# Norm sums made on all partitions, and four sums moved behind a mask, in a two-layer hybrid trunk

## The chip, the cores and the metric

The kernel runs on one core of a Trainium2 chip. The metric is the device time of one execution in microseconds (us). A core has a matrix engine (TensorE, in the profile PE, with its weight loads as PEld), a vector engine (VectorE, DVE), a scalar engine (ScalarE, ACT) that evaluates functions such as Exp or Sqrt from tables it has to load, GpSimd (POOL), and SyncE (SP), which here only issues DMA transfers. Data lie in SBUF with 128 partitions; TensorE writes its products to PSUM banks of 128 x 512 fp32, and a bank can take a new product only when the old one has been read. Every engine works through its own instructions in a fixed order, so an instruction that waits holds up all behind it on that engine.

## The reference

The input is x with 1024 tokens of 1024 channels, fp32. Cut to what matters here:

```python
def rmsnorm(x, g):
    return x * rsqrt(mean(x * x, axis=-1) + EPS) * g

# layer 0: S5 state-space branch with GLU, and retention, each times its gate
u, g_s5, q, k, v, g_ret = split(rmsnorm(x, norm_g[0]) @ w_in_ab)
y_s5 = glu(gelu(s5(u))) * silu(g_s5)
y_ret = retention(q, k, v) * silu(g_ret)      # 8 heads, chunks of 64 tokens
x = x + concat([y_s5, y_ret]) @ w_out_ab

# layer 1: convolution module
a, b, g = split(rmsnorm(x, norm_g[1]) @ w_in_c)
u = depthwise_causal_conv(a * sigmoid(b), width=31) + conv_b
u = (u - mean(u)) * rsqrt(var(u) + EPS) * ln_g + ln_b
x = x + (silu(u) * silu(g)) @ w_out_c

out = rmsnorm(x, final_g)
```

All means run over the 1024 channels of a token. There are three RMS norms and one layer norm over channels (the "conv norm").

## The kernel before

Everything is held with channels on the partitions and tokens along the free dimension: 8 blocks of 128 channels, and two halves of 512 tokens (`HALF`). Each weight product is done as three fp32r products, high x high, high x low and low x high (`mm3`, lines L181 to L183), so one 128 x 512 output block over 1024 channels is 24 matrix products. Norm factors are one number per token. Because the tokens lie along the free dimension, a factor must stand on all 128 partitions, as a 128 x 512 tile, before a block can be multiplied by it.

The order of instructions on each engine is chosen by a scheduler from the program's order, from priorities (`self.at(...)`) and from explicit orderings (`issue_after`). Two names of such orderings are used to hold back weight products until a norm's matrix products have been placed: `self.last_stat` (the last sum) and `self.last_spread` (the last spread).

How a norm's factor is made. ScalarE squares the blocks, GpSimd or VectorE adds the squares of the 8 blocks, which leaves one 128 x 512 tile that must still be summed over the partitions.

- `token_sums` (L444): each 128 x 128 part of that tile is the stationary operand and 64 columns of ones move, in plain fp32. One instruction is two MATMULs in the profile. The sum of token t comes out on partition t, so 512 tokens become a 128 x 4 tile.
- `rsqrt` (L453, L454): Sqrt on ScalarE with its own table, reciprocal on VectorE, on that small tile.
- `spread_split` (L461 to L473) puts the 4 columns on all partitions: they are split into a high and a low part, VectorE multiplies the identity by each (two diagonal 128 x 512 tiles, `dg`), and two fp32r products with ones add them up. `spread` (L480, L483) does it with one plain fp32 diagonal.

Where it happens:

- Layer 0's front (`layer0_front`): the sums of all 1024 tokens (tile `ss`) after the first step of the second half of the u2 product; the factors R (L335) for both halves after two spreads; `Rtok`, the same factors with tokens on partitions, is a by-product that the values of retention use. Then `u_block(nb)` multiplies finished products by R (`ut`, L356, "eviction"), and SP stores each `ut` to `u_d` (L364). `ut` has 2 buffers, so block 2 must wait until block 0's store has read its buffer. The products themselves have three rotating banks beside those of u0 and u1; the second half of u3 takes the bank of u2's first half, and so waits for its eviction. The S5 parameter steps (`s5t`, 128 x 32 and 128 x 64) are VectorE work between them, and the low part of u5's weights (`wl_u`, L172) too.
- Layer 1's norm, for each half (`h1`, names r_ps, r_R), the conv norm for each half (`conv_norm`, cst for its sums of values and of squares, cR for the factor and cD for mean times factor), and the final norm (`final_norm`, rf_ps, rf_R): the first half whole, the second half in two quarters of 256 tokens. For the last quarter `IDLE` products keep TensorE going and the factor is spread twice (rf_R and rf_C).

Retention runs in four pairs of heads (`ret_heads`). For each pair: keys are transposed, kv products per chunk (L1116), the state S chained over the chunks on VectorE (L1124, L1126), scores sp (L1133), masked by VectorE into sc (L1139) in two halves `hf`, then the output ro from S (L1160) and from the masked scores (L1165), statistics (L1174), and transposes back (rt). Beside each pair, `y_pass(rq, pair)` carries a part of the S5 output y through DMA, Gelu, a store to `yn_d`, four in-place sums on VectorE (L917 to L920), and after a `yield` a split into high and low parts with stores to `t_d`. The sums are written in place, so they must wait until the `yn_d` store has read the tiles. For the pairs 1 and 2 the split comes behind the second masked scores.

## Time and profile before

| what | value |
| --- | --- |
| median of 3 runs | 1183.63 us (1182.59 to 1185.37) |
| the profiled execution | 1188.26 us, of which its span is 1186.5 us |
| mean granted TensorE clock | 0.995 of full speed |
| TensorE busy | 1173.5 us (99%), 6326 instructions |
| VectorE busy | 851.1 us (72%), 1479 instructions |
| GpSimd busy | 657.4 us (55%), 448 instructions |
| ScalarE busy | 483.6 us (41%), 712 instructions |
| ScalarE's table loads | 12.8 us in 10 |

A profile page counts in us from the start of the span. In a timeline a row is: start, duration, engine, line, operation, output<-inputs, shapes, and in brackets the idle time before it with what ended it; "x4" says that four equal instructions are drawn together, and their duration is that of the whole group. In the chain of waits a row is start, duration, and what the time went to. Matrix products overlap: one starts before the modelled end of the one before, so costs are taken from starts. The granted clock is the share of TensorE's full speed that its throttle allowed.

### The profile page before, as it was taken

The numbers are of one execution on the slowest core, as the hardware profiler recorded it, in microseconds if no ns is written. First come the engines' busy times: TensorE is split into PE (matmuls) and PEld (weight loads), VectorE is DVE, ScalarE is ACT, GpSimd is POOL, SyncE is SP. The second block draws the span as 40 slices with busy tenths as digits, with TensorE's granted clock in tenths as the row PEclk, the third lists the DMA queues.
The fourth block names the chain that finished last, engine by engine and source line by source line (L and its number), as shares of the span: only waits on it lengthen the run. The fifth ranks groups of instructions, "written<-read, shape, count | busy, mean of one in ns | idle before, by whom it ended". The sixth has DMA issues, their size and how long they took to land.

```text
span 1186.5 us, 17318 instructions
## 1 busy us (share of the span) xinstructions
PE 1173.5 (99%) x6326; PEld 985.8 (83%) x6326; DVE 851.1 (72%) x1479; ACT 483.6 (41%) x712; POOL 657.4 (55%) x448
## 2 busy tenths in 40 slices
PE   9999999999999999899999999999999999999997
PEld 7888888888888889889888888888888888888886
DVE  7975698777427458476679422699999999989743
ACT  6322232222222231333546322545435676434662
POOL 2059999888145354232574110678444567767753
PEclk9999999999999999999999999999999999999999
DMA  9344355565387676759998987655668754357874
GB/s 355 107 129 136 131 156 167 182 186 170 109 280 280 233 231 181 259 177 343 371 344 290 336 266 254 213 198 196 227 243 280 231 180 166 107 189 253 268 246 145
DMA packets 117637, 261.46 MB, mean 220 GB/s; under 512 B 10672, under 2 KB 42288, under 8 KB 116912
## 3 DMA queue, kind: packets, MB, share of 16 engines
q1 hardware_dynamic: 117552, 260.36, 65.4%
q8 instruction: 49, 0.80, 0.3%
q14 instruction: 36, 0.29, 0.1%
HBM read 181.48 MB, written 74.65 MB: 216 GB/s over the span
## 4 chain that ended last, share of the span: by engine, by line
PE 93%; DMA 3%; DVE 2%; issue 1%; SPq 0%; POOL 0%; ACT 0%; POOLq 0%; DVEq 0%; ACTq 0%
PE mm_g L181 8%; PE mm_g L183 7%; PE mm_g L182 7%; PE mm_wo L182 5%; PE mm_wo L181 5%; PE mm_wo L183 5%; PE mm_b L182 2%; PE mm_b L183 2%; PE mm_a L183 2%; PE mm_a L182 2%; PE mm_b L181 2%; PE mm_a L181 2%; PE mm_oc L181 2%; PE mm_oc L183 2%; PE mm_oc L182 2%; PE mm_u L183 2%
## 5 line engine op out<-in xcount | busy, mean ns | idle before, releaser
L1467 DVE SCALAR_TENSOR_TENSOR cv<-u,convw,cv 128x512 f32<-128x512 f32 x398 | 273.7, 751 | 9.0 <-ACT cv L1450 6.9
L1444 POOL TENSOR_TENSOR tp<-tp,tp 128x512 f32<-128x512 f32 x64 | 83.7, 1307 | 35.2 <-ACT tp L1443 34.0
L181 PE MATMUL mm_g<-xh,wh_g 128*128 128x512 f32 x256 | 101.8, 398 | 0.0
L183 PE MATMUL mm_g<-xh,wl_g 128*128 128x512 f32 x256 | 100.1, 391 | 0.0
L182 PE MATMUL mm_g<-xl,wh_g 128*128 128x512 f32 x256 | 100.0, 391 | 0.0
L415 POOL TENSOR_TENSOR s1q<-s1q,s1q 128x512 f32<-128x512 f32 x12 | 17.7, 1478 | 85.2 <-ACT s1q L410 85.2
L1443 ACT ACTIVATE tp<-u,convw 128x512 f32<-128x512 f32 x64 | 45.6, 719 | 37.3 <-POOL tp L1444 35.8
L181 PEld LDWEIGHTS mm_g<-xh,wh_g 128*128 128x128 f32 x256 | 48.0, 188 | 11.7 <-issue 1.2
L183 PEld LDWEIGHTS mm_g<-xh,wl_g 128*128 128x128 f32 x256 | 48.1, 188 | 10.4
L182 PEld LDWEIGHTS mm_g<-xl,wh_g 128*128 128x128 f32 x256 | 48.1, 188 | 9.9 <-issue 0.4
L371 DVE TENSOR_TENSOR gt<-mm_g,R 128x512 f32<-128x512 f32 x32 | 21.9, 684 | 46.5 <-PE mm_g L183 46.4
L172 POOL TENSOR_TENSOR wl_glu<-wf_glu,wh_glu 128x1024 fp32r<-128x1024 f32 x14 | 34.0, 2428 | 33.8 <-ACT wh_glu L171 33.2
L183 PE MATMUL mm_oc<-zh,wl_woc 128*128 128x512 f32 (+1 forms) x144 | 52.5, 366 | 0.0
L172 POOL TENSOR_TENSOR wl_v<-wf_v,wh_v 128x1024 fp32r<-128x1024 f32 x12 | 31.1, 2601 | 38.5 <-ACT wh_v L171 38.5
L182 PE MATMUL mm_oc<-zl,wh_woc 128*128 128x512 f32 (+1 forms) x144 | 52.5, 366 | 0.0
L181 PE MATMUL mm_oc<-zh,wh_woc 128*128 128x512 f32 (+1 forms) x144 | 52.3, 369 | 0.0
L181 PE MATMUL mm_g<-h1h,wh_cg 128*128 128x512 f32 x128 | 49.9, 390 | 0.0
L181 PE MATMUL mm_wo<-ysh,wh_wos 128*128 128x512 f32 x128 | 49.9, 390 | 0.0
L182 PE MATMUL mm_b<-h1l,wh_cb 128*128 128x512 f32 x128 | 49.9, 390 | 0.0
L183 PE MATMUL mm_g<-h1h,wl_cg 128*128 128x512 f32 x128 | 49.8, 389 | 0.0
L181 PE MATMUL mm_b<-h1h,wh_cb 128*128 128x512 f32 x128 | 49.8, 389 | 0.0
L182 PE MATMUL mm_a<-h1l,wh_ca 128*128 128x512 f32 x128 | 49.8, 389 | 0.0
(506 smaller groups left out, 3663.6 us busy)
## 6 DMA issues: line engine op xcount, KB each, us to landing
wf_g<-w_ab SPq DMA_DIRECT2D x16, 512.0 KB
wf_wos<-w_out SPq DMA_DIRECT2D x16, 512.0 KB
wf_wor<-w_out SPq DMA_DIRECT2D x16, 512.0 KB
wf_cb<-w_c SPq DMA_DIRECT2D x16, 512.0 KB
wf_ca<-w_c SPq DMA_DIRECT2D x16, 512.0 KB
wf_woc<-w_out_c SPq DMA_DIRECT2D x16, 512.0 KB
wf_v<-w_v SPq DMA_DIRECT2D x12, 512.0 KB
wf_cg<-w_c SPq DMA_DIRECT2D x11, 512.0 KB
```

Of the source, the lines that this page charges most:

```text
L172: self.low_made = lo[i].tensor_tensor(wl[:].rearrange(fl)[:, c], wf[:, c], h.bitcast(F32), op=ALU.subtract)
L181: nc.tensor.matmul(ps, wh[:, kb, :], xh, start=start, stop=False, **more)
L182: nc.tensor.matmul(ps, wh[:, kb, :], xl, start=False, stop=False, **more)
L183: self.last_mm = nc.tensor.matmul(ps, wl[:, kb, :], xh, start=False, stop=stop, **more)
L371: nc.vector.tensor_tensor(gt[:, c], ps[:], self.R[:, c], op=ALU.mult)
L415: nc.gpsimd.tensor_tensor(a, a, sq[:], op=ALU.add)
L1443: nc.scalar.mul(sk[:], u[:, k:k + HALF], cw[:, nb, k:k + 1])
L1444: gp.tensor_tensor(s0[:], s0[:], sk[:], op=ALU.add)
L1467: v.scalar_tensor_tensor(dst[:], *tap, accs_[i][:], op0=ALU.mult, op1=ALU.add)
```

## The change

All norms but the last quarter of the final one get their sums on all partitions at once: `wide_sums` has a 128 x 128 tile of ones as the stationary operand and moves the 128 x 512 tile of added squares in plain fp32, so each of the 128 output partitions has the sum of every token. `wide_rsqrt` then works on whole tiles: ScalarE does Ln, Exp with scale -0.5, and Square; VectorE does one Newton step in two `scalar_tensor_tensor` passes. It loads the table for Ln and Exp ahead (not for the first half of the conv norm, `table=bool(h)`). The diagonal tiles, the spreads, the tiny `rsqrt` tiles of these norms, and the orderings that held products back for a spread are removed. The conv norm has one bank each for the two sums, and mean times factor is made by one VectorE pass. In the front, the two halves are summed and made into R one after the other, behind the first and the second step of the second half of u2; `Rtok` now comes by DMA: R's first row is written to a new DRAM tile `r_d` and read back as 128 x 8. Both stand on SP's queue ahead of the stores of `ut`. The last quarter keeps the old way (`rstd_last`), with its Sqrt table loaded after the third quarter's Square.

In `y_pass` a second `yield` stands ahead of the four sums. For all pairs but the third (`pair == 2`) the caller goes on at once, as before; for the third, `ret_heads` calls `scored()` after the first half's masks, and there the four sums are issued, behind the first mask.

```diff
@@ -28,11 +28,10 @@
-RMM = 5
-NORM_TAPS = (23, 24), (11, 12)
+NORM_TAP = 23, 11
@@ -214,14 +213,13 @@
-        self.mhalf = self.cp.tile([P, KB], F32, name="mhalf")
-        nc.vector.memset(self.mhalf[:], -0.5)
+        self.r_d = dt("r_d", [1, T])
@@ -262,7 +260,7 @@
-            nc.scalar.activation(sq[:], xt[kb][:], AF.Square)
+            self.squared = nc.scalar.activation(sq[:], xt[kb][:], AF.Square)
@@ -319,26 +317,21 @@
         self.R = self.mid.tile([P, T], F32, name="R0")
         self.Rtok = self.mid.tile([P, 8], F32, name="Rtok")
-        rps = acc[1]
         w_u2 = self.wnext("u2")
         u2 = [self.bank(f"mm_u2_{h}", aux=False) for h in range(2)]
         self.gemm(u2[0][:], w_u2, xs[0])
-        u2_step = lambda kb: self.mm3(u2[1][:], w_u2, kb, (xs[1][kb][0][:], xs[1][kb][1][:]), kb == 0, kb == KB - 1)
-        u2_step(0)
-        with self.tc.issue_after(self.last_mm.ins):
-            self.token_sums([(rps, ssum[:])])
-        self.rsqrt(self.Rtok[:], rps[:].rearrange("p (b x) -> p b x", x=64)[:, :, 0], 1.0 / D)
-        for h in range(2):
-            rp = acc[h]
-            self.spread_split(rp[:], self.Rtok[:, 4 * h:4 * h + 4], ev, f"r0_{h}", (("dg", 2), ("sq", 2)), True)
-            nc.scalar.copy(self.R[:, h * HALF:(h + 1) * HALF], rp[:])
-        r_diag = self.last_diag
-        for kb in range(1, KB):
-            with self.tc.issue_after(self.last_spread.ins) if kb >= RMM else nullcontext():
-                u2_step(kb)
+        for kb in range(KB):
+            self.mm3(u2[1][:], w_u2, kb, (xs[1][kb][0][:], xs[1][kb][1][:]), kb == 0, kb == KB - 1)
+            if kb < 2:
+                c = slice(kb * HALF, (kb + 1) * HALF)
+                with self.tc.issue_after(self.last_mm.ins):
+                    self.wide_sums(acc[kb][:], [ssum[:, c]])
+                self.wide_rsqrt(acc[kb][:], ev, f"r0_{kb}", 1.0 / D, self.R[:, c], bufs=2)
+        r_ready = self.last_newton
+        nc.sync.dma_start(self.r_d[:], self.R[0:1, :])
+        nc.sync.dma_start(self.Rtok[:], self.r_d[0].rearrange("(b p) -> p b", p=P))
         def scaled(nb, w, name, cb):
             for h in range(2):
@@ -376,7 +369,7 @@
-        with self.tc.issue_after(xdma.ins), self.tc.issue_after(r_diag.ins):
+        with self.tc.issue_after(xdma.ins), self.tc.issue_after(r_ready.ins):
@@ -436,78 +429,72 @@
-    def token_sums(self, terms):
...
-    def rsqrt(self, dst, src, scale=1.0, pool=False):
...
+    def wide_sums(self, ps, parts):
+        for i, a in enumerate(parts):
+            self.last_stat = self.nc.tensor.matmul(ps, self.ones[:], a, start=i == 0, stop=i == len(parts) - 1)
+    def wide_rsqrt(self, src, pool, name, scale=1.0, dst=None, copy=None, bufs=1, table=True):
+        nc, v, n = self.nc, self.nc.vector, src.shape[1]
+        half = pool.tile([P, HALF], F32, name=f"{name}_ha", tag="sq", bufs=bufs)[:, :n]
+        y = copy
+        if y is None:
+            y = pool.tile([P, HALF], F32, name=f"{name}_y", tag="dg", bufs=bufs)[:, :n]
+        dst = src if dst is None else dst
+        after = self.squared
+        if table:
+            with self.tc.issue_after(after.ins):
+                after = nc.scalar.preload_act_table_set("natural_log_exp_and_others")
+        with self.tc.issue_after(after.ins):
+            nc.scalar.activation(y, src, AF.Ln, scale=scale, bias=self.epst[:])
+        nc.scalar.activation(y, y, AF.Exp, scale=-0.5)
+        self.halved = nc.scalar.activation(half, y, AF.Square, scale=(0.5 * scale) ** 0.5)
+        v.scalar_tensor_tensor(src, src, EPS / scale, half, op0=ALU.add, op1=ALU.mult)
+        self.last_newton = v.scalar_tensor_tensor(dst, src, 1.5, y, op0=ALU.subtract, op1=ALU.mult, reverse0=True)
+        if copy is not None:
+            nc.scalar.copy(copy, dst)
+    def rsqrt(self, dst, src, scale=1.0):
-    def spread_split(self, ps, r4, pool, name, slots=(("dg", 1), ("sq", 1)), low_scalar=False):
...
-    def spread(self, ps, r4, pool, name, tag="dg", bufs=1, more=()):
...
-    def rstd(self, parts, pool, name, idle=0):
...
+        root = nc.scalar.activation(dst, src, AF.Sqrt, scale=scale, bias=self.epst[:])
+        nc.vector.reciprocal(dst, dst)
+        return root
+    def rstd(self, parts, pool, name, copy=None, table=True):
+        n = parts[0].shape[1]
+        ps = self.bank(f"{name}_R")
+        self.wide_sums(ps[:, :n], parts)
+        self.wide_rsqrt(ps[:, :n], pool, name, 1.0 / D, copy=copy, table=table)
+        return ps
+    def rstd_last(self, parts, pool, name):
+        with self.tc.issue_after(self.halved.ins):
+            nc.scalar.preload_act_table_set("sqrt_and_others")
+        ps, wait, *rp = (self.bank(f"{name}_{k}", aux=False) for k in ("ps", "wait", "R", "C"))
+        terms = [(b, a[:, b * P:(b + 1) * P]) for a in parts for b in range(nb)]
+        for i, (b, a) in enumerate(terms):
+            last = nc.tensor.matmul(ps[:, b * 64:(b + 1) * 64], a, self.ones[:, :64], start=i == 0, stop=i == len(terms) - 1)
+        with self.tc.issue_after(last.ins):
+            for _ in range(IDLE):
+                last = nc.tensor.matmul(wait[:, :P], self.ones[:], self.ones[:], start=True, stop=True)
+        dg = pool.tile([P, 4, P], F32, name=f"{name}_dg", tag="sq", bufs=1)[:, :nb, :]
+        nc.vector.tensor_tensor(dg, self.ident[:].unsqueeze(1).broadcast_to([P, nb, P]),
+                                r4.unsqueeze(2).broadcast_to([P, nb, P]), op=ALU.mult)
+        with self.tc.issue_after(last.ins):
+            for o in rp:
+                nc.tensor.matmul(o[:, :n], self.ones[:], dg.rearrange("p b t -> p (b t)"), start=True, stop=True)
@@ -913,6 +900,7 @@
+        yield
@@ -972,14 +960,22 @@
                     held.enter_context(self.tc.issue_after(self.last_rs.ins))
                 parts = self.y_pass(rq, pair)
                 next(parts)
+                if pair != 2:
+                    next(parts)
                 if pair in (0, 3):
                     next(parts, None)
+            def scored():
+                if pair == 2:
+                    with self.tc.issue_after(self.masked[0].ins):
+                        next(parts)
             def turned():
                 if pair == 3:
                     early.close()
                     self.lp = self.pool("l1", side="right")
-            self.ret_heads(pair, *cur, V, turned)
+            self.ret_heads(pair, *cur, V, turned, scored)
             if pair < 3:
                 with self.tc.issue_after(self.masked[1].ins):
@@ -1139,6 +1135,8 @@
                 self.masked[hf] = v.tensor_tensor(
                     sc[hh][:, 4 * hf:4 * hf + 4, :], sps[hh][:].rearrange("p (b i) -> p b i", b=4),
                     mask[:, hh, :].unsqueeze(1).broadcast_to([P, 4, P]), op=ALU.mult)
+            if hf == 0:
+                scored()
         gts = []
@@ -1459,11 +1457,11 @@
-                    ahead = [x for x, k0 in zip(self.norm_first, NORM_TAPS[i]) if (h, n2) == (0, 6) and k >= k0]
+                    ahead = (h, n2) == (0, 6) and k >= NORM_TAP[i]
-                    with self.tc.issue_after(ahead[-1].ins) if ahead else nullcontext():
+                    with self.tc.issue_after(self.norm_first.ins) if ahead else nullcontext():
@@ -1511,30 +1509,23 @@
         def conv_norm(h):
             sm, acc = accs[("cv", h)]
-            st = ps_cv.tile([P, HALF], F32, name=f"cst_{h}", tag="cn")
+            s1, s2 = (ps_cv.tile([P, HALF], F32, name=f"cst{i}_{h}", tag="cn") for i in range(2))
             q7 = csquare(h, 7)
-            s1, s2 = st[:, 0:256], st[:, 256:512]
             e = v if h else gp
             e.tensor_tensor(sm[:], sm[:], cv[h][7][:], op=ALU.add)
             e.tensor_tensor(acc[:], acc[:], q7[:], op=ALU.add)
-            self.token_sums([(s1, sm[:]), (s2, acc[:])])
-            st4 = st[:].rearrange("p (k b x) -> p k b x", k=2, x=64)
-            t4 = [lp.tile([P, 4], F32, name=f"cn4_{i}_{h}", tag=f"cn4_{i}", bufs=1) for i in range(4)]
-            d4, q4, v4, r4 = (t[:] for t in t4)
-            nc.scalar.activation(q4, st4[:, 0, :, 0], AF.Square, scale=1.0 / D)
-            nc.scalar.mul(d4, st4[:, 0, :, 0], 1.0 / D)
-            v.scalar_tensor_tensor(v4, st4[:, 1, :, 0], 1.0 / D, q4, op0=ALU.mult, op1=ALU.subtract)
-            self.rsqrt(r4, v4)
-            v.tensor_tensor(d4, d4, r4, op=ALU.mult)
-            Rp = ps_cv.tile([P, HALF], F32, name=f"cR_{h}", tag="cn")
-            self.spread_split(Rp[:], r4, lp, f"cR_{h}")
-            Dp = ps_cv.tile([P, HALF], F32, name=f"cD_{h}", tag="cn")
-            with self.tc.issue_after(self.last_diag.ins):
-                self.spread_split(Dp[:], d4, lp, f"cD_{h}", (("tp", 3),) * 2 if h else (("dg", 1), ("sq", 1)))
-            self.norm_mm[h] = self.last_stat, self.last_spread
+            self.wide_sums(s1[:], [sm[:]])
+            first = self.last_stat
+            self.wide_sums(s2[:], [acc[:]])
+            self.norm_mm[h] = first, self.last_stat
+            m2 = lp.tile([P, HALF], F32, name=f"cm2_{h}", tag="dg", bufs=1)
+            self.squared = nc.scalar.activation(m2[:], s1[:], AF.Square, scale=1.0 / D)
+            v.scalar_tensor_tensor(s2[:], s2[:], 1.0 / D, m2[:], op0=ALU.mult, op1=ALU.subtract)
             R = lp.tile([P, HALF], F32, name=f"RL_{h}", tag="cq", bufs=1)
+            self.wide_rsqrt(s2[:], lp, f"cn_{h}", copy=R[:], table=bool(h))
+            Rp = s2
             dl = lp.tile([P, HALF], F32, name=f"dl_{h}", tag="cs", bufs=1)
             for nb in range(8):
                 c = cv[h][nb]
@@ -1543,8 +1534,7 @@
-                    nc.scalar.copy(R[:], Rp[:])
-                    nc.scalar.copy(dl[:], Dp[:])
+                    v.scalar_tensor_tensor(dl[:], s1[:], 1.0 / D, R[:], op0=ALU.mult, op1=ALU.mult)
@@ -1591,13 +1581,15 @@
-            rp = self.rstd([final[h][nb][1][:, c] for nb in ((0, KB - 1) if end else (0,))], lp, f"rf_{h}_{c.start}",
-                           IDLE if end else 0)
+            if end:
+                rp, copied = self.rstd_last([final[h][nb][1][:, c] for nb in (0, KB - 1)], lp, f"rf_{h}_{c.start}")
+            else:
+                rp = self.rstd([final[h][0][1][:, c]], lp, f"rf_{h}_{c.start}", R[:, :n], h == 0)
-                if nb == (4 if end else 1):
-                    nc.scalar.copy(R[:, :n], (self.copied if end else rp)[:, :n])
+                if end and nb == 4:
+                    nc.scalar.copy(R[:, :n], copied[:, :n])
@@ -1615,17 +1607,16 @@
-        self.hold = {4: self.last_stat, 8: self.last_spread}
+        self.hold = {4: self.last_stat}
-        self.norm_first = self.last_sum, self.last_diag
+        self.norm_first = self.last_sum
-            gates((0,), range(G0), {0: {4: self.last_stat, 7: self.last_spread}, 1: {0: self.last_spread},
-                                  2: {0: self.last_spread}})
+            gates((0,), range(G0), {0: {4: self.last_stat}, 1: {0: self.last_stat}, 2: {0: self.last_stat}})
@@ -1655,8 +1646,8 @@
-                stat, spread = self.norm_mm[1]
-                blocks(0, range(N0, 8), {N0: {HOLD: stat}, N0 + 1: {0: spread}})
+                first, stat = self.norm_mm[1]
+                blocks(0, range(N0, 8), {N0: {HOLD: stat}, N0 + 1: {0: stat}})
@@ -1671,10 +1662,9 @@
-                sums, spread = self.last_stat, self.last_spread
+                sums = self.last_stat
-                among.update({0: sums, 3: spread})
+                among.update({0: sums})
```

More of the change, by code (lines that the diff above doesn't have):

```diff
@@ L437, in at @@
         return cm()
-    def token_sums(self, terms):
-        terms = [(ps[:, b * 64:(b + 1) * 64], a[:, b * P:(b + 1) * P]) for ps, a in terms
-                 for b in range(a.shape[1] // P)]
-        for i, (o, a) in enumerate(terms):
-            self.last_stat = self.nc.tensor.matmul(o, a, self.ones[:, :64], start=i == 0, stop=i == len(terms) - 1)
-    def rsqrt(self, dst, src, scale=1.0, pool=False):
-        nc = self.nc
-        if pool:
-            nc.vector.tensor_scalar(dst, src, scale, EPS, op0=ALU.mult, op1=ALU.add)
-            nc.gpsimd.tensor_tensor(dst, dst, self.mhalf[:, :dst.shape[1]], op=ALU.pow)
-        else:
-            root = nc.scalar.activation(dst, src, AF.Sqrt, scale=scale, bias=self.epst[:])
-            nc.vector.reciprocal(dst, dst)
-            return root
@@ L1086, in ret_values_wide, with ret_heads @@
         return lambda p, b, hh: res[b // 4][:, b % 4, (2 * p + hh) * P:(2 * p + hh + 1) * P]
[L1088 removed]
+    def ret_heads(self, pair, K, Q, qadds, mask, kdec, V, turned, scored):
         nc, rp = self.nc, self.rp
```

43 lines of the change are left out of this document (2 added, 41 removed).

## The prediction

> **What bounds the kernel now.** I read the page first: busy time, the chain that ended last, the costliest groups.
>
> ```profile
> PE 1173.5 (99%) x6326; PEld 985.8 (83%) x6326; DVE 851.1 (72%) x1479; ACT 483.6 (41%) x712; POOL 657.4 (55%) x448
> ...
> PE 93%; DMA 3%; DVE 2%; issue 1%; SPq 0%; POOL 0%; ACT 0%; POOLq 0%; DVEq 0%; ACTq 0%
> ...
> L1467 DVE SCALAR_TENSOR_TENSOR cv<-u,convw,cv 128x512 f32<-128x512 f32 x398 | 273.7, 751 | 9.0 <-ACT cv L1450 6.9
> ```
>
> TensorE sets the time: it is busy for 99% and the chain runs on it for 93%. So what counts is TensorE work added or removed, and TensorE's waits. VectorE, at 72%, is nearest to it where the taps of the depthwise convolution run (the last row: 398 of them, with 9.0 us of idle time before them). The view of PE's waits has few (total, times, longest), the largest and the smallest of them:
>
> ```profile
> PE sp L1133 <- DVE S L1126: 3.5, 1, 3.5
> ...
> PE mm_u L181 <- DVE ut L356: 0.3, 1, 0.3
> ```
>
> The first is in the third pair's retention pass, the other in the front, where layer 0's first factors are made. The change touches both. Two views of the first, the chain from 490 us and the granted clock in half microseconds (last three numbers of a row: clock, DMA share, GB/s):
>
> ```profile
> 492.74 6.02 DMA yn_d<-yn
> ...
> 498.88 0.70 DVE yn L917
> ...
> 503.25 1.83 PE sp L1133 x13
> ...
> 505.29 1.42 PE ro L1160 x11
> 506.71 3.29 PE ro L1165 x16
> ```
> ```profile
> 499.50:500.00 0.50, 0.26 (x2) 0.00 (x0) 0.47 (x2) 0.00 (x0) 0.00 (x0) 1.00 0.67 270
> ...
> 502.50:503.00 0.50, 0.00 (x0) 0.00 (x0) 0.46 (x2) 0.00 (x0) 0.00 (x0) 0.57 0.00 0
> ...
> 509.00:509.50 0.50, 0.50 (x5) 0.50 (x5) 0.50 (x4) 0.00 (x0) 0.00 (x0) 0.60 1.06 426
> ```
>
> The four sums of y wait for a DMA until 498.88 and take 0.70 each. The S chain stands behind them on VectorE, and TensorE stands still for 3.5 us before 503.25. Its clock halves at about 502.7, 3.0 us into the stop, and is back at about 509.1, 5.9 us after work resumed. So this wait costs twice. The same work of an earlier pair, at full clock, and, from TensorE's timeline, the start of the weight products ahead of the third pair's sp:
>
> ```profile
> 406.47 0.97 PE sp L1133 x13
> ...
> 407.56 0.67 PE ro L1160 x11
> 408.23 1.98 PE ro L1165 x16
> ```
> ```profile
> 496.48 0.50 PE L181 MATMUL mm_k<-xh,wh_k 128*128 128x512 f32 x1
> ```
>
> The slow clock cost (1.83 - 0.97) + (1.42 - 0.67) + (3.29 - 1.98) = 2.92 us on top of the 3.5.
>
> **Third pass: the four sums behind the first masked scores.** S then needs only kv, which TensorE has behind it before 496.48, so S is ready near 498. In the changed order nine mm_k products (0.23 each) stand ahead of the rest of sp, which starts near 498.6. Both losses go: -3.5 - 2.9 = -6.4. What is late next is the second half's masked scores: on VectorE they queue behind three of the sums, which still start at 498.88, and kraw between them. Three sums, kraw and two masks at 0.65 to 0.70 end at 502.3 (first mask) and 503.0 (second). TensorE has sp and the first half's ro to do, 0.97 + 0.67 + 1.98 = 3.6 us, so to 502.2, and then needs the two banks that the masks free. I price that new wait at 0.6 (0.1 to 0.9: one bank or both). ScalarE has nothing in this; the fourth sum feeds only transposes some 12 us later. Term: **-5.8** (-6.3 to -5.0).
>
> **The norms' sums.** Chain rows of the old way, sums (L444) and spreads (L473), and one row of a plain fp32 product, 256 wide, which is two MATMULs:
>
> ```profile
> 906.46 0.84 PE r_ps L444 x8
> 909.43 0.53 PE r_R L473 x2
> ...
> 1110.36 1.73 PE cst L444 x16
> 1116.96 0.47 PE cR L473 x2
> ...
> 1178.87 0.70 PE L483 MATMUL rf_R<-rf_dg,ones 128*128 128x256 f32 x2
> 1179.40 0.59 PE L483 MATMUL rf_C<-rf_dg,ones 128*128 128x256 f32 x2
> ```
>
> No row shows a plain fp32 product 512 wide. The nearest is the last pair: MATMULs that last 0.379 start 0.21 apart (0.59 - 0.38), so 256 wide costs 0.42 and 512 wide twice that, 0.85. From below: two MATMULs at the spacing of an fp32r one of the same width (0.23: two in 0.47, the cR row) cost 0.45. From above: the rf_R row is followed 0.53 later, which doubled is 1.06. I take 0.85, the same number format. Then each layer-1 norm half and the last norm's first half saves 0.84 + 0.49 - 0.85 = about 0.48 (three: -1.4); each conv norm half has two sums and two spreads, 1.73 + 2 x 0.47 - 1.70 = 0.97 (two: -1.9); the third quarter of the last norm about 0.4. Together **-3.7**; 7.5 wide products outside the front make the ends -6.7 and -2.1.
>
> Cover: the new factor is three ScalarE passes and two VectorE passes over a whole tile, some 0.6 and 0.7 each, about 3.2 us, against tiny passes and diagonal tiles before, a similar length. TensorE covers it with weight products of the other half or the next stage, as it did; without that cover a norm would stop TensorE for those 3.2 us. For the second conv norm the margin is small, by VectorE's timeline:
>
> ```profile
> 1109.35 0.68 DVE L1520 TENSOR_TENSOR cq<-cq,cvq 128x512 f32<-128x512 f32 x1
> ```
>
> The last add ends at 1110.03, the sums run at 1110.36. With the saving of about 2 us ahead of it TensorE would arrive there before VectorE, which has the taps to do. I put 0.5 for these places together (0 to 2).
>
> **The front.** These are VectorE's, TensorE's, ScalarE's and SP's timelines:
>
> ```profile
> 38.99 0.42 DVE L549 TENSOR_SCALAR s_s_ci<-s_s_ci 128x512 f32<-128x512 f32 x1
> ...
> 40.26 0.09 DVE L657 MEMSET s_e2i<- 128x32 f32 x1
> ...
> 40.99 2.17 DVE L356 TENSOR_TENSOR ut<-mm_u,R 128x512 f32<-128x512 f32 x2
> ...
> 45.33 1.24 DVE L172 TENSOR_TENSOR wl_u<-wf_u,wh_u 128x1024 fp32r<-128x1024 f32 x1
> 46.47 0.66 DVE L565 SCALAR_TENSOR_TENSOR s5t<-s5t,s5t 128x32 f32<-128x32 f32 x3
> 47.44 2.17 DVE L356 TENSOR_TENSOR ut<-mm_u,R 128x512 f32<-128x512 f32 x2 [0.31 <-DMA u_d<-ut]
> ```
> ```profile
> 34.89 1.96 PE L444 MATMUL ss<-ones,ssum 128*128 128x64 f32 x16
> ...
> 39.48 1.41 PE L473 MATMUL ss<-r_dg,ones_r 128*128 128x512 f32 x4
> ...
> 48.71 0.47 PE L181 MATMUL mm_u<-xh,wh_u 128*128 128x512 f32 x1 [0.34 <-DVE ut L356]
> ```
> ```profile
> 33.38 1.04 ACT L171 CAST wh_u<-wf_u 128x1024 fp32r<-128x1024 f32 x1
> 34.88 1.28 ACT L453 ACT_TABLE_LOAD   x1 [0.46 <-DVE ssum L268]
> ...
> 40.37 1.15 ACT L335 COPY R<-ss 128x512 f32<-128x512 f32 x2
> ```
> ```profile
> 44.33 1.43 SPq L364 DMA_DIRECT2D u_d<-ut  x2
> ```
>
> Before, two u evictions run at 40.99, two at 43.18 and the fifth at 47.44, once the u_d store (issued 44.33, landed 3.1 later) has freed its buffer; TensorE needs that fifth one for a bank and waits 0.34. In the changed program's order the factor comes in halves. ScalarE: table load to 34.8, the cast to 35.8, three passes of 0.58 to about 37.7. VectorE then, in order: two Newton passes (1.4, to 39.1), two evictions (2.2, to 41.3), the second half's Newton passes (to 42.7), the stretch from s_s_ci to the memsets (38.99 to 40.3, so 1.3, to 44.0), wl_u (1.1, to 45.1), the other two evictions (46.2 and 47.3), fourteen small S5 steps at 0.19 (to 50.0), and only then the fifth eviction, which also needs the store of the first pair. That store is issued near 46.6, behind the new write of r_d and read of Rtok and behind wf_g on SP: it lands at 49.7 if those cost nothing, near 51 if wf_g's 512 KB go ahead. So the fifth eviction runs from between 50.0 and 51 for 1.1 us, and TensorE goes on near 51.8 instead of 48.71: +3.1 (2.5 to 3.6). TensorE itself saves here 1.96 + 1.41, less 0.2 each because the next product starts before the last one's end, less the two wide sums' 1.7: 1.3. That only makes it run dry earlier, at 46.9 where it was 48.2: the stop is 4.9 us.
>
> The third pass lost its clock 3.0 us into a stop of 3.5, so one of 4.9 should lose it too, for another 2.9. Term: **+6.0** (2.5 without the clock's fall, 7 with all late).
>
> The Trainium skill, "TensorE: Matmul & The Clock Gate", section "Part 1: The HAM clock gate", says that the clock halves after one idle window of some 3.4 us and that the windows run freely. By that, a stop of 4.9 holds a whole window in (4.9 - 3.4)/3.4, under half of the cases. The trace has it fall after 3.0 us, which does not bear a full window out; no run here shows where the windows lie.
>
> **The tail.** VectorE and ScalarE at the end:
>
> ```profile
> 1176.20 0.42 DVE L1580 TENSOR_TENSOR x<-mm_oc,x1l 128x256 f32<-128x256 f32 x1 [0.18 <-PE mm_oc L183]
> 1176.54 1.08 DVE L1610 TENSOR_TENSOR fo<-x,rf_R 128x256 f32<-128x256 f32 x3
> 1178.12 0.17 DVE L454 RECIPROCAL rf_r<-rf_r 128x2 f32<-128x2 f32 x1 [0.50 <-ACT rf_r L453]
> ```
>
> Before, three of the six fo multiplications stand ahead of the last add of x and three behind. After, all six stand behind it: 1176.54 + 6 x 0.36 = 1178.7, where the reciprocal of the last quarter stood at 1178.12, with everything after it. Term: **+0.6** (0 to 1). ScalarE has the extra table load (1.28) there, over by about 1176.2, before the last square.
>
> **Sum**: -5.8 - 3.7 + 0.5 + 6.0 + 0.6 = -2.4 against the profiled run of 1188.26 (span 1186.5 and 1.8 around it). The median is 1183.63, 4.6 lower; the same 2.4 off it gives 1181.2. The ends of all terms together give -10.5 to +2.9; they are unlikely to meet.
>
> **Rivals.**
> 1. The front's stop does not halve the clock, or the wait is shorter. For: halving depends on what a window sees, and only one stop of this length is in the trace. Against: that one, the shorter, did halve it. -2.4 - 2.9 = -5.3: 1178.3; with the low ends of some other terms down to 1175. By the rule of the Trainium skill above this would be as likely as the forecast.
> 2. Slower: the store of the first u pair is held up by the round trip through r_d. Place: SP's queue between 42.7 and 47. Price: Rtok is 1024 single elements, and SP issues it only when r_d has landed; yn_d took 6.02 from issue to landing against 3.1 of u_d, so landings do stretch. Each microsecond that u_d lands after 50.5 goes to the end: the gain is gone from a landing at 52.9, and it is slower by 0.2% from 55.3. At 56, 5.5 late: +3.1, 1186.7. Against: r_d is 4 KB, and the queue is nearly empty there before.
> 3. The norms' savings are given back, because VectorE in the conv stage has to catch up. The 3.7 is lost: +1.3, 1184.9. Against: the 9.0 us of idle time before its taps.
> 4. The change does not do what it says: the third pass's wait moves to the second mask at full size, the clock falls as before. For: the sums still start at 498.88. Against: TensorE has 3.6 us of work in between. The gain shrinks from 5.8 to about 1: +2.4, 1186.0.
>
> **How the numbers follow.** About 0.2% (2.4 us) is what a measurement of this kernel can tell from no change. Forecast 0.50, its own range 1177.5 to 1184.5: 0.27 faster, 0.20 within, 0.03 slower. Rival 1 0.24, all faster. Rival 2 0.14: 0.12 slower, 0.02 within. Rival 3 0.06: 0.05 within, 0.01 slower. Rival 4 0.06: 0.04 slower, 0.02 within. Together faster 0.51, same 0.29, slower 0.20. The range goes from rival 1's low end to just beyond rival 2: 1175 to 1187.
>
> **What would show it.** Right: no PE wait at sp L1133 in the third pass and a clock of 1.00 around 500 to 510; a PE wait on ut of 4 to 5.5 us near 47 to 52, with granted clock 0.5 after it; wide sums 0.85 apart for 512; the last reciprocal 0.6 later. Wrong: the front's wait under 3 us (then rival 1 or better), or over 8 (rival 2); a new wait at L1165's bank over 1 us; sums of 512 that cost 0.45 or over 1; PE waits at the conv norms.

## The result, and the profile after

The changed kernel took 1190.05 us (median of 6 runs, 1188.82 to 1191.05), the kernel before 1183.66 us (6 runs beside them); the ratio is 1.005, interval 1.0037 to 1.0063. So it is slower by about 6 us, outside the range given, and on the other side of the forecast. The profiled execution took 1191.05 us, span 1189.2, mean granted clock 0.992.

The view of PE's waits after, with its columns as before (total, times, longest):

```profile
PE mm_u L180 <- DVE ut L349: 4.9, 1, 4.9
PE cst L435 <- DVE cs L1516: 3.9, 1, 3.9
...
PE rf_R L497 <- DVE rf_dg L493: 0.7, 1, 0.7
```

The wait on S in the third pass is gone. Two large waits are new: the one in the front, as forecast to the tenth, and one at the second conv norm's sums, where the forecast had put 0.5 us.

The front after, first the granted clock by windows (busy times, then clock, DMA share, GB/s), then VectorE's timeline:

```profile
50.00:51.00 1.00, 0.00 (x0) 0.00 (x0) 0.86 (x6) 0.00 (x0) 0.00 (x0) 0.97 1.15 348
51.00:52.00 1.00, 0.00 (x0) 0.00 (x0) 0.31 (x2) 0.00 (x0) 0.00 (x0) 0.50 1.14 344
...
57.00:58.00 1.00, 1.00 (x4) 0.81 (x3) 1.00 (x10) 0.00 (x0) 0.00 (x0) 0.62 0.00 0
```
```profile
40.52 2.17 DVE L349 TENSOR_TENSOR ut<-mm_u,R 128x512 f32<-128x512 f32 x2
...
46.31 2.12 DVE L349 TENSOR_TENSOR ut<-mm_u,R 128x512 f32<-128x512 f32 x2
...
50.92 0.17 DVE L516 TENSOR_SCALAR s5t<-s_s_prm 128x32 f32<-128x32 f32 x1
51.78 2.06 DVE L349 TENSOR_TENSOR ut<-mm_u,R 128x512 f32<-128x512 f32 x2 [0.69 <-DMA u_d<-ut]
```

The fifth eviction, at 47.44 before, stands at 51.78 behind the S5 steps and the store of u block 0, which was still on its way 0.69 us after VectorE was ready. The clock halves at 50.9, 2.9 us into the stop, and is whole again at 57.8. Laid beside the profile of before by their matrix products, the after trace is 4.3 us late when TensorE goes on at 52.99, 6.5 late behind 57.8, and still 6 late in retention. Of this, 1.1 us are there at 33 us already, before the change bears, so the front costs 5.4 to 5.5.

The second conv norm, VectorE, GpSimd, and the chain there:

```profile
1108.44 0.69 DVE L1570 TENSOR_TENSOR x<-mm_oc,x1l 128x512 f32<-128x512 f32 x1 [0.86 <-PE mm_oc L182]
1109.05 0.74 DVE L1465 SCALAR_TENSOR_TENSOR co<-u,convw,cv 128x512 f32<-128x512 f32 x1
1109.89 2.39 DVE L1516 TENSOR_TENSOR cs<-cs,co 128x512 f32<-128x512 f32 x1
1112.20 1.75 DVE L1517 TENSOR_TENSOR cq<-cq,cvq 128x512 f32<-128x512 f32 x1
```
```profile
1109.38 2.35 POOL L171 TENSOR_TENSOR wl_woc<-wf_woc,wh_woc 128x1024 fp32r<-128x1024 f32 x1 [1.19 <-ACT wh_woc L170]
1111.69 1.72 POOL L1575 TENSOR_TENSOR s2q<-s2q,s2q 128x512 f32<-128x512 f32 x1
```
```profile
1112.34 3.72 PE cst L435 x4
```
```profile
1112.00:1113.00 1.00, 0.66 (x1) 0.40 (x2) 1.00 (x2) 0.00 (x0) 1.00 (x1) 0.74 0.84 332
1113.00:1114.00 1.00, 1.00 (x2) 0.00 (x0) 0.95 (x1) 0.00 (x0) 0.40 (x1) 0.50 1.06 328
...
1115.00:1116.00 1.00, 1.00 (x3) 0.46 (x2) 0.00 (x0) 1.00 (x1) 0.00 (x0) 0.55 0.78 291
```

The add of x (L1570) waits for TensorE's last product block, and the last tap, cs and cq stand behind it; the sums of the conv norm, which TensorE comes to next, need cs and cq. So TensorE stops at 1108.4 and waits until VectorE has done the first three of these four operations; cq follows while the sum of cs runs. Two of the four are long: cs and cq take 2.39 and 1.75 us, and each ends 0.5 us after the GpSimd operation that it overlaps (1111.73 and 1113.41). The clock is at half from 1112.5 to 1115.9, and the four MATMULs of the two sums take 3.72 us, where one such sum of two MATMULs in the front took 0.87 (below). Before, cs and cq stood ahead of that add of x, and TensorE did not wait (cq, between these two, is in the prediction):

```profile
1108.04 1.39 DVE L1519 TENSOR_TENSOR cs<-cs,co 128x512 f32<-128x512 f32 x1
...
1110.40 0.69 DVE L1580 TENSOR_TENSOR x<-mm_oc,x1l 128x512 f32<-128x512 f32 x1 [0.37 <-PE mm_oc L183]
```

What the forecast had right shows in these rows of the after trace: a wide sum in the front, from the chain; the pair's work in the third pass at full clock; and the tail, where the six fo and the reciprocal now follow the last add of x:

```profile
36.12 0.87 PE ss L435 x2
```
```profile
504.82 0.97 PE sp L1129 x13
505.90 0.67 PE ro L1158 x11
506.57 1.98 PE ro L1163 x16
```
```profile
1177.40 0.42 DVE L1570 TENSOR_TENSOR x<-mm_oc,x1l 128x256 f32<-128x256 f32 x1 [0.15 <-PE mm_oc L182]
1178.04 2.08 DVE L1602 TENSOR_TENSOR fo<-x,rf_R 128x256 f32<-128x256 f32 x6 [0.21 <-ACT RF L457]
1180.03 0.16 DVE L463 RECIPROCAL rf_r<-rf_r 128x2 f32<-128x2 f32 x1
```

One thing does not fit: the two profiled executions are only 2.8 us apart (1191.05 and 1188.26), the medians 6.4. The profiled run of before was 4.6 above its own median.

### The profile page after: what moved, and what is told of

It is laid out like the page before. It is cut to its first block, busy times and chain, and to the rows that moved or that the text cites. A ratio compares the mean times of both kernels' runs of the same rounds, so it can differ in the third digit from the quotient of the medians.

```text
span 1189.2 us, 17134 instructions
## 1 busy us (share of the span) xinstructions
PE 1170.7 (98%) x6250; PEld 977.9 (82%) x6250; DVE 855.5 (72%) x1452; ACT 492.0 (41%) x716; POOL 654.8 (55%) x448
## 4 chain that ended last, share of the span: by engine, by line
PE 88%; DMA 6%; DVE 2%; ACT 1%; issue 1%; POOL 0%; SPq 0%; POOLq 0%; DVEq 0%
PE mm_g L180 8%; PE mm_g L181 7%; PE mm_g L182 7%; PE mm_wo L181 5%; PE mm_wo L182 5%; PE mm_wo L180 5%; PE mm_a L180 2%; PE mm_b L180 2%; PE mm_b L181 2%; PE mm_a L182 2%; PE mm_a L181 2%; PE mm_b L182 2%; PE mm_oc L181 2%; PE mm_oc L180 2%; PE mm_oc L182 2%; PE mm_u L181 2%
## 5 line engine op out<-in xcount | busy, mean ns | idle before, releaser
L180 PE MATMUL mm_u<-xh,wh_u 128*128 128x512 f32 x128 | 50.5, 406 | 5.2 <-DVE ut L349 4.9
L182 PE MATMUL mm_b<-h1h,wl_cb 128*128 128x512 f32 x128 | 50.6, 395 | 0.0
L181 PE MATMUL mm_u<-xl,wh_u 128*128 128x512 f32 x128 | 50.4, 397 | 0.1
```

What stands on the lines that cost most here:

```text
L180: nc.tensor.matmul(ps, wh[:, kb, :], xh, start=start, stop=False, **more)
L181: nc.tensor.matmul(ps, wh[:, kb, :], xl, start=False, stop=False, **more)
L182: self.last_mm = nc.tensor.matmul(ps, wl[:, kb, :], xh, start=False, stop=stop, **more)
```

## The experiments

Times are medians, and ratios are against the kernel before on the same chip. The kernel before itself scatters there (its medians in the three series were 1187.45, 1183.36 and 1185.21); what that is, the first two runs show. The changed kernel (1190.05) was not run again in these series, so a difference to it sets two series side by side.

**1. The kernel before once more.** No edit.

> The kernel before, unchanged, with a profile of its own. The profiled run shown before took 1188.26 us, 4.6 above the median of 1183.66. Theory A (the third pair's stop of 3.5 us and the slow clock behind it, 6.4 us together, are in every run): the stop on S is 3 to 4 us again, with a granted clock of 0.5 behind it. Theory B (the stop depends on when one store lands, and that first profiled run was an unlucky one): a run within 1.5 us of 1183.7 has a stop under 2.5 us and no slow clock around 500 to 510 us.

Measured: 1185.58 us (1182.41 to 1191.32 in 12 runs), ratio 0.9995 (0.9976 to 1.0015); its profiled run took 1183.80. The chain of that run around the third pass, and the clock:

```profile
490.74 4.30 DMA yn_d<-yn
495.17 0.70 DVE yn L917
...
500.70 0.61 DVE sc L1139
501.35 0.93 PE ro L1160 x10
```
```profile
501.00:502.00 1.00, 0.81 (x13) 0.65 (x10) 1.00 (x3) 0.00 (x0) 0.00 (x0) 1.00 0.00 0
```

No wait on S, only 0.2 us of TensorE on sc, and a clock of 1.00. The store of yn was issued 2.0 us earlier than in the first profile (490.74, there 492.74) and landed in 4.30 us instead of 6.02: 3.7 us together, which is the stop of 3.5. In the first profile an earlier store on the same queue (yr_d) had taken 7.9 us to land and held up the load ahead of this one:

```profile
484.37 7.94 DMA yr_d<-grl
492.32 0.32 SPq L1148
```

The two profiles, 1188.26 and 1183.80, differ by 4.5 us: laid side by side, the first loses 6.1 us on the second in the third pass, and gains 1.1 where the second waits 0.8 us in the GLU:

```profile
PE mm_glu L181 <- DVE mm_gluz L1334: 0.8, 1, 0.8
```

Of 95 executions of the kernel before in the series, 49 lie under 1185 us (half of these under 1183.5, called the better runs below) and 46 between 1185 and 1191.3. Only two of them have a profile. The mean granted clock is known for 89: it is 0.998 or 0.999 in all 45 that lie under 1185, and 0.995 or 0.996 in 16 of the 17 above 1188.8, so the longest runs had a stop that cost them the clock. That it was this stop is shown for one run, and argued for the rest from run 2. Theory B holds: the loss is a matter of when stores land; why one lands late is open.

**2. Only the third pass.** On the kernel before:

```diff
         (b11, b12), (b21, b22) = ((y[:, :HALF], y[:, HALF:]) for y in yns)
         v = nc.vector
+        yield
...
                 next(parts)
+                if pair != 2:
+                    next(parts)
                 if pair in (0, 3):
                     next(parts, None)
+            def scored():
+                if pair == 2:
+                    with self.tc.issue_after(self.masked[0].ins):
+                        next(parts)
```

> The kernel before with only the four sums of the third pair moved behind the first masks; all norms as before. Theory A: -5 to -6.4 us, ratio 0.9946 to 0.9958. Theory B: the profiled run of before overstated the loss by its 4.6 us, so -1 to -3 us, ratio 0.9975 to 0.999. In both, no PE wait on S in the third pass.

Measured: 1183.12 us, and above all 1181.98 to 1184.94 in all 12 runs; ratio 0.9969 (0.9955 to 0.9983). There is no wait on S, and the granted clock is 0.998 or 0.999 in all 12. The ratio lies between the two expectations (A from 0.9946 to 0.9958, B from 0.9975 to 0.999), so neither has the size: both spoke of medians, and the median of before in this series (1187.45) is one of a late store. The move takes away the upper half of the scatter (up to 1191.3) and leaves the lower one as it is: the better runs of before, at 1182 to 1184, gain nothing. Against the median shown with the kernel before, 1183.66, which lies among those, the move is worth about 0.5 us, not 5.8; this run's profile gains 0.4 us in the third pass on that of run 1. How far the changed kernel lies behind depends on this too: 6.4 us against 1183.66, but 2.6 against 1187.45.

**3. Only the norms.** The changed kernel, with `scored` empty and the four sums in their old place.

> The changed kernel with the four sums of the third pair back in their old place; all norms as in the changed kernel. Theory A: 6.4 + 6 = +12 us against the kernel before, ratio 1.0105. Theory B: 6.4 + 2 = +8 to +9.5 us, ratio 1.007 to 1.008, since the move gave only 1 to 3.

Measured: 1193.08 us, ratio 1.0056 (1.0036 to 1.0076). Against the better runs of before (1183.5) that is +9.6, against that series' median (1187.45) +5.6. Its profile (1196.08, the longest of the six runs) has the stops of 5.0 and 3.9 us, one of 2.1 on a load in the S5 stage and one of 1.8 on S. So the move is worth about 3 us on top of the norms, as theory B had it.

**4. The front the old way.** The changed kernel, with the front's lines of before back (sums by token behind step 0, two spreads, Rtok from `rsqrt`):

```diff
-            if kb < 2:
-                    self.wide_sums(acc[kb][:], [ssum[:, c]])
-                self.wide_rsqrt(acc[kb][:], ev, f"r0_{kb}", 1.0 / D, self.R[:, c], bufs=2)
+            self.token_sums([(rps, ssum[:])])
+        self.rsqrt(self.Rtok[:], rps[:].rearrange("p (b x) -> p b x", x=64)[:, :, 0], 1.0 / D)
...
+            self.spread_split(rp[:], self.Rtok[:, 4 * h:4 * h + 4], ev, f"r0_{h}", (("dg", 2), ("sq", 2)), True)
```

> The changed kernel with layer 0's front made the old way (sums by token, two spreads, Rtok without a round trip). The two traces put the front's cost at +6.3 us by the turn of the S5 stage (104.29 against 97.76, less the part before 36 us). If that is right in all runs: 6.4 - 6.3 = about 0 against the kernel before, -1 to +1 (ratio 0.999 to 1.001). Rival: later waits take up part of the delay, so undoing it gives back under 4 us: +2.4 or more, ratio over 1.002.

Measured: 1185.97 us (1184.57 to 1187.17), ratio 0.9993 (0.998 to 1.0006). It gives back 4.1 us against the changed kernel, between the two expectations, and is still some 2.5 us above the better runs of before. Laid beside the undisturbed profile of before, this trace is 1.3 us ahead at 700, of which 1.1 are the wait in the GLU that run 1's profile has and this one has not. It gains 0.5, 0.6 and 1.1 us at the next three norms (1.8 ahead by 757, 3.5 by 961 us) and loses all of it at the second conv norm (0.3 behind at 1114). The largest of PE's waits is that stop; no other is over 1.1:

```profile
PE cst L467 <- DVE cs L1548: 3.9, 1, 3.9
```

**5. The order at the second conv norm.** The add of x for the last block is put behind cq:

```diff
-            e.tensor_tensor(acc[:], acc[:], q7[:], op=ALU.add)
+            summed = e.tensor_tensor(acc[:], acc[:], q7[:], op=ALU.add)
+            if h:
+                self.chained([self.add4], summed)
```

> The changed kernel with one ordering added: the add of x that follows the last product block ahead of the second conv norm's sums is put behind the two adds that those sums need (cs, cq). In the changed kernel's trace that add stands ahead of the last tap and of cs and cq on VectorE, waits for the block to end at 1108.4, and TensorE then waits 3.9 us for cs, and has the slow clock for about 3 us after. If that order is the cause: the stop shrinks to 0.5 to 2 us and the slow clock goes, so -3 to -5.4 us against the changed kernel, to 1185 to 1187. Rival (VectorE is simply behind with its taps): less than -1 us, and the stop stays above 3.

Measured: 1190.25 us, ratio 1.0054 (1.0036 to 1.0072): no gain. A miss, and the trace shows why:

```profile
1107.55 0.69 DVE L1516 TENSOR_TENSOR cs<-cs,co 128x512 f32<-128x512 f32 x1
1109.02 2.33 DVE L1517 TENSOR_TENSOR cq<-cq,cvq 128x512 f32<-128x512 f32 x1 [0.78 <-ACT cvq L1484]
```
```profile
PE cst L435 <- DVE cq L1517: 2.0, 1, 2.0
...
PE cst L435 <- DVE cs L1516: 0.8, 1, 0.8
```
```profile
1111.00:1112.00 1.00, 0.59 (x1) 0.50 (x2) 0.96 (x2) 0.35 (x1) 0.00 (x0) 0.57 0.61 242
```

cs is early now, but cq waits for ScalarE's square and then runs 2.33 us beside a GpSimd operation. Two stops, 0.8 and 2.0, take the place of one of 3.9, and the clock falls all the same. So the order explains part of the stop only. The rest is TensorE's lead, ScalarE's square and the long cq; no run sets GpSimd's part in it apart.

**6. A buffer of its own for u block 2.**

```diff
-            ut = uv.tile([P, 8, P], F32, name=f"ut_{nb}", tag="ut", bufs=2)
+            ut = (ev.tile([P, 8, P], F32, name=f"ut_{nb}", tag="xin", bufs=8) if nb == 2 else
+                  uv.tile([P, 8, P], F32, name=f"ut_{nb}", tag="ut", bufs=2))
```

> The changed kernel with a buffer of its own for u block 2, so that its eviction no longer waits for the store of block 0. VectorE then evicts block 2's first half right behind block 1's, near 43 us. If the fifth eviction's place is what stops TensorE in the front: no stop on ut there and no slow clock, -5.5 to -6.8 us against the changed kernel, to 1183.3 to 1184.6. Rival: another wait takes its place (block 3's bank, the later start of the S5 steps): less than -3 us.

Measured: 1183.26 us, ratio 0.999 (0.9976 to 1.0005), so -6.8 against the changed kernel: the upper end. Three evictions now follow each other, and TensorE has no wait on ut left:

```profile
39.92 3.23 DVE L350 TENSOR_TENSOR ut<-mm_u,R 128x512 f32<-128x512 f32 x3
```

The fifth eviction's place sets the front's loss, all of it: in this profile the front is 2.1 us shorter than in run 1's, where the changed kernel's is 5.4 longer.

**7. Both repairs (5 and 6).**

> Both repairs together, with the moved sums of the third pair: if the two losses are separate, their gains add up: -8.5 to -12 us against the changed kernel, 1178 to 1181.5, below the kernel before also where that one does not stop (1183). Rival: TensorE only reaches the next wait earlier and the gains overlap: above 1182.

Measured: 1181.80 us, ratio 0.9978 (0.9963 to 0.9993). Just outside the expectation (1178 to 1181.5), and short of the rival's 1182: the order gives 1.5 us here (1183.26 to 1181.80), and the stops of 0.8 and 2.0 stay.

**8. TensorE kept busy in the front's stop.**

```diff
+                    fb = self.bank("fill")
+                    with self.tc.issue_after(self.last_mm.ins):
+                        for _ in range(16):
+                            self.fill = nc.tensor.matmul(fb[:, :P], self.ones[:], self.ones[:], start=True, stop=True)
```

> The changed kernel with 16 small products of ones (128 x 128, written to a bank nobody reads) put into TensorE's stop in the front, so that the stop stays but TensorE is busy for most of it. It prices the clock alone: if the slow clock behind the stop costs its share (from 52.99 to 57.4 us the delay grows from 4.3 to 6.3), -1.5 to -2.3 us against the changed kernel and a granted clock of 1.00 from 51 to 58. If the clock has no part in the loss: 0, or up to +0.5 if the products outlast the stop.

Measured: 1193.01 us, ratio 1.0072 (1.0046 to 1.0098). Inconclusive for the clock: in the profiled run the store of block 0 landed later than in any other (VectorE waited 2.9 us for it), so that 3.6 us of idle time remained behind the filling products, and the clock fell.

**9. Work put ahead of the second conv norm's sums.**

```diff
-N0, HOLD = 5, 1
+N0, HOLD = 5, 5
```

> The changed kernel with HOLD 5 for 1: four steps of the next product block (about 3 us) now stand ahead of the second conv norm's sums on TensorE, so that TensorE has work while VectorE finishes the last tap, cs and cq. Theory: TensorE reaches these sums 2.5 to 3 us earlier against VectorE than before the change, because the norms before it cost TensorE less, and that lead (and the slow clock behind the stop) is all that is lost there: the stop of 3.9 goes under 1 and the clock stays at 1.00, so -4 to -5.4 us against the changed kernel, 1184.6 to 1186. Rival: whatever TensorE does ahead, the norm's own chain is late and TensorE waits for z afterwards: less than -2 us, with a new wait on z or at the next blocks.

Measured: 1188.27 us (1186.75 to 1189.76), ratio 1.0021 (1.0006 to 1.0037): -1.8 against the changed kernel, so the rival has it in size, and each has half of the mechanism. The stop and the slow clock at the sums are gone, cs and cq take 0.69 each with GpSimd idle beside them, and TensorE leaves the sums 4.3 us earlier than in the changed kernel (1.1 of this it had before them). But it then waits for z, the normed blocks:

```profile
1107.34 0.69 DVE L1516 TENSOR_TENSOR cs<-cs,co 128x512 f32<-128x512 f32 x1
1108.00 0.69 DVE L1517 TENSOR_TENSOR cq<-cq,cvq 128x512 f32<-128x512 f32 x1
```
```profile
PE mm_oc L180 <- ACT zh L1196: 2.4, 2, 1.5
...
PE mm_oc L181 <- POOL zl L1198: 0.9, 1, 0.9
```

**10. The buffer and the hold together.**

> The changed kernel with both: the buffer of its own for u block 2 and HOLD 5. If the two stops are all that the change lost: 1183.3 - 4.5 = 1178 to 1180, and below the run with both earlier repairs (1181.8). Rival: 1181 or more, if the lead of TensorE is only lost at a later wait.

Measured: 1179.94 us (1179.49 to 1181.0, 6 runs), ratio 0.9946 (0.9926 to 0.9966). It beats both kernels: the changed one by 10 us, the one before by 5 in this series' median and by about 3.5 against its better runs. The waits on z (3.3 us) are the largest that it has left.

**11. The round trip of R behind the stores of u.** `r_d` and `Rtok` are issued behind the stores of blocks 0 and 1:

```diff
+            if nb == 1:
+                put = nc.sync.dma_start(self.r_d[:], self.R[0:1, :])
+                get = nc.sync.dma_start(self.Rtok[:], self.r_d[0].rearrange("(b p) -> p b", p=P))
+                self.chained([put, get], self.u_store)
```

> The changed kernel with the round trip of R through r_d put behind the stores of u blocks 0 and 1 on SP's queue. In the changed kernel's trace the first store was issued 0.1 us after its eviction and landed 4.3 us later, against 3.1 before; VectorE was free for the fifth eviction 0.7 us before it landed. If the round trip's 1024 single elements held the store up: landing again near 3.1 us, the fifth eviction starts near 51.1 and not 51.8, -0.5 to -1 us. If it has no part in the store's time: no difference beyond noise (within 0.5).

Measured: 1189.04 us, ratio 1.0032 (1.0017 to 1.0047), 1.0 below the changed kernel. But in the trace the store still lands 4.4 us after its issue:

```profile
46.71 1.38 SPq L355 DMA_DIRECT2D u_d<-ut  x2
...
51.12 2.06 DVE L347 TENSOR_TENSOR ut<-mm_u,R 128x512 f32<-128x512 f32 x2 [0.78 <-DMA u_d<-ut]
```

The round trip has no part in it. What stretches the store from 3.1 to 4.4 us was not tried apart; the load of wf_g, which stood behind the first store before and now stands ahead of it, is the nearest candidate.

## Why the prediction was wrong, point by point

Two steps failed, the third pass and the second conv norm. The table lays the after profile (1191.05) beside that of run 1 (1183.80), in which no store was late, by the start of the same matrix products. It says how much later the after profile gets in each stretch, and what the prediction had for it; its 0.5 for uncovered norm chains is put at the second conv norm.

| stretch, by run 1's time | measured, us | forecast, us |
| --- | --- | --- |
| to 33 us, before the change bears | +0.56 | |
| the front, to 70 | +5.36 | +6.0 |
| from there to 480 | -0.26 | |
| third pass, to 540 | -0.42 | -5.8 |
| GLU, to 700 (run 1's wait of 0.8) | -0.33 | |
| layer 1's norm, two halves, and the first conv norm, to 970 | -2.20 | -1.9 |
| second conv norm and the blocks behind it, to 1145 | +4.29 | -0.5 |
| last norm, to the last quarter's sums | -1.22 | -0.9 |
| tail, to the end | +1.56 | +0.6 |
| sum | +7.34 | -2.4 (rounded) |

- **The third pass** is the first step that failed. The mechanism was right: no wait on S and no slow clock; against the first profile of before the pass gains 6.5 us (the after trace is 6.0 behind at 490 and 0.5 ahead at 530). But the prediction took the 6.4 us of one profile for a property of the kernel and subtracted 5.8 from a median that did not hold it. It had the warning in its own table: the profiled run was 4.6 us above the median, and it moved the sum over with "the same 2.4 off it". Runs 1 and 2 show it: worth 0.4 to 0.5 us where the store is in time, and 6.1 to 6.5 where the traces set the late store beside a timely one.
- **The second conv norm** is the other. The prediction put 0.5 (0 to 2) on it against a saving of 0.97, and on balance it lost 4.3. In this are a stop of 3.9 us, some 1.7 for the clock (3.4 us at half speed; an estimate from the trace) and 0.7 in the blocks behind; against them stand the spreads that are gone. This is rival 3 with a clock behind it: VectorE's chain sets when the sums can start, so that the 2.2 us TensorE saved at the three norms before are lost there, and a stop that brings the clock down costs more than was saved. The prediction saw the thin margin (0.3 us) and the lead of 2 us but not that the add of x had changed places with the last tap, cs and cq, nor that GpSimd would run beside them. Runs 5 and 9 show that the order and the lead each have a part; run 9 also shows that with both gone, and GpSimd's overlap with cs and cq too, the norm's chain stops TensorE later, for 3.3 us on z.
- **The front** was right: a stop of 4.9 us, as worked out; 1.4 saved by TensorE ahead of it, where 1.3 were forecast; 2.2 us for the clock where 2.9 were priced; 5.4 in place of 6.0. Run 6 shows that the place of the fifth eviction is the whole cause. Rival 1 (the clock stays) falls: in all six profiles with a stop of 3.6 to 5.3 us there (the changed kernel and runs 3, 5, 8, 9 and 11) it fell. Rival 2 (the round trip) falls with run 11.
- **The norms' sums** were right in price: 0.87 for a 512-wide sum where 0.85 was estimated. The three norms from layer 1's to the first conv norm gave 0.5, 0.6 and 1.1 us, where 0.48, 0.48 and 0.97 were forecast.
- **The tail** cost 1.6 where 0.6 was priced. By the mechanism given it is 0.7: against the first profile of before, 1.2 us late at the last quarter's first sums (1177.20 against 1176.00), and 1.9 at the reciprocal (1180.03 against 1178.12). The other 0.9 are a slow clock from 1180.75 on, under the last two products (0.70 and 0.59 us before, where the clock fell only behind them, at 1181.83):

```profile
1180.70 1.21 PE L497 MATMUL rf_R<-rf_dg,ones 128*128 128x256 f32 x2 [0.73 <-DVE rf_dg L493]
1181.70 1.06 PE L497 MATMUL rf_C<-rf_dg,ones 128*128 128x256 f32 x2
```

The 7.3 us of the table are those of two executions; the medians differ by 6.4 (1190.05 and 1183.66), and the 0.9 between them are within the scatter of both kernels.

## What to carry to other kernels

Look first at how far the profiled execution lies above the median: a wait that ends on a DMA may belong to that execution, and removing it narrows the scatter more than it moves the better runs. Time saved on the bounding engine is kept only until the next place where another engine's chain decides; work it through that place, and ask which instruction there has changed its order. And add the slow clock to the price of a stop of a few microseconds: here 2.9 us behind a stop of 3.5, 2.2 behind one of 4.9, some 1.7 behind one of 3.9. Work placed ahead of such a wait removes both, but only as far as the chain behind it allows: run 9 took away the stop of 3.9 and its clock and gained 1.8 us.

## What the hardware showed beside

The granted clock changes on a grid. In the after trace it changes at 50.94, 57.77, 1112.48, 1115.90 and 1180.75 us: 6.83, 1054.71, 3.42 and 64.85 apart, which is 2, 309, 1 and 19 steps of 3.413. The other profiles have the same steps, each from a start of its own. The clock can fall behind a shorter stop than 3 us: in run 5 TensorE stopped for 0.8 us, worked for 1.1, stopped for 2.0, and the granted clock was at 0.57 in the microsecond in which it went on; in run 3 a single stop of 2.1 us was enough (it fell at 248.71), while stops of 1.5 us in runs 9 and 10 were not. And how long it stays low depends on where the stop lies on the grid: one step where work went on before the fall or at most 0.6 us behind it (run 11: fall at 52.14, work from 52.34, full clock at 55.55), two where it went on later (after: 50.94, 52.99, 57.77). The prediction read 502.7 and 509.1 off rows of the first profile that give 502.57 and 509.40.

The Trainium skill, "TensorE: Matmul & The Clock Gate", section "Part 1: The HAM clock gate", has the clock fall after an idle window of about 3.4 us, on windows that run freely. The traces agree with the length of the windows and their free start. If an idle window is one without any product, as the prediction took it, they do not agree: the step that ended with the fall had 0.5 us of work in it at 50.94, 0.6 at 502.57 before, and 1.1 in run 5.

VectorE's adds of two SBUF tiles took 0.69 us with GpSimd idle (run 9), and 2.39, 1.75 and 2.33 us beside GpSimd operations, ending 0.5 us after those did. The Trainium skill, "SBUF — State Buffer", section "SBUF: two separate sides", says that the two engines share one pair of ports that one of them holds for a whole instruction, also against a VectorE operation with two SBUF inputs if the GpSimd one reads SBUF. The trace agrees: 1109.38 + 2.35 = 1111.73, and cs ended at 1112.28. Before, too, cs met a GpSimd operation, which ended at 1108.87, and took 1.39 us, to 1109.43.
